# Weight halves, a fused mask and maximum, float32r sums of squares and a new order in a one-core hybrid decoder layer

## The chip, the cores and the metric

The kernel runs on one core of a Trainium2 chip. The metric is the device time of one execution in microseconds (us), as a median over runs. The engines are called as in the profile: PE (TensorE, matmuls), PEld (its weight loads), DVE (VectorE), ACT (ScalarE), POOL (GpSimd) and SP (SyncE, which here issues nearly all DMAs).

## What is computed

One decoder layer on 512 tokens of width 1024, all in float32. Cut to what matters:

```python
def swiglu(h, wg, wu, wd):
    return (jax.nn.silu(h @ wg) * (h @ wu)) @ wd          # inner width 2816
...
    x = x + 0.5 * swiglu(rms_norm(x, ffn1_norm), ffn1_wg, ffn1_wu, ffn1_wd)
    h = rms_norm(x, mix_norm)
    (q_n, kc, vc, ksl, vsl, kwn, vwn, gts, q_s, k_s, v_s) = jnp.split(h @ w_in, split_at, axis=-1)
    o_nsa = nsa_mixer(...)        # 8 heads: compressed + selected + window attention, gated, masked softmax
    o_sb = stick_breaking(q_s, k_s, v_s)                  # 8 heads, no softmax
    x = x + jnp.concatenate([o_nsa, o_sb], axis=-1) @ w_out
    x = x + memory_cross_attention(rms_norm(x, mem_x_norm), rms_norm(mem, mem_kv_norm), ...)   # 4 heads
    x = x + 0.5 * swiglu(rms_norm(x, ffn2_norm), ffn2_wg, ffn2_wu, ffn2_wd)
```

## The kernel before

Activations lie transposed in SBUF: eight tiles of 128 features by 512 tokens. A float32 operand is split into a high and a low float32r part: ACT copies the high part, DVE subtracts it from the source (`wsplit`, `split`), and a product is three float32r passes (`mm3`: high by high, high by low, low by high).

The work has three stretches. First comes a start written out by hand (`FIRST`): five plain blocks of the first feed-forward network (`ffn_up`) and the operands of its Winograd form (`right`: differences of the quarters b11, b12, b21, b22 of the activations). Then the rest of that network follows by `FEED["1"]`: a bare number f is one Winograd block of 128 inner columns (`wino_up`: seven products of 12 matmuls with 256 columns, four sums of weight quarters), `c.j` is a down step (`ffn_down`: group c of blocks into output tile j), and `name:i` is a store (`store_parts`: a weight unit that the middle will need is loaded, split and written to DRAM as parts). Groups of blocks are set by `GROUPS`. Then comes the middle by `MIDDLE` (projections, stick-breaking heads, NSA scores and outputs, memory attention, output projections, and `gate.f`, early halves of the second network's blocks), and last the second network by `FEED["2"]`.

None of this is issued in the order of the code. A `Planner` records every instruction with a cost in ns and its dependencies, and then lists them engine by engine by priority, under the limits of buffers and PSUM banks (`SYNC_NS`, `DMA_NS`, `ACT_MORE` and the `cost` function are its prices). Whatever it decides is the fixed order of each engine's queue. All instructions are issued from one line of `emit` (L498), so that the profile tells them apart by tile names: `raw` are weights as loaded, `w` split weights, `t` the tiles of 512, `p` PSUM, `d` parts in DRAM, `c` and `cr` constants (float32 and float32r), `s` small columns, `half` two intermediate sums of a Winograd block.

Places that the change touches: raw weights are loaded as tiles of 1024 columns, four buffers (`load`, `NRAW`); weight sums go into fresh `w` tiles (`comb` in `wino_up`); `norm_rstd` and `head_norm` sum squares over partitions with one float32 matmul by ones from `c`; `nsa_scores` adds the causal mask by a matmul of the identity with `R_NSM` and takes the maximum with `tensor_reduce` from PSUM; `cmp_mlp` builds the compression input in one raw tile and splits it in two halves of 512.

Of the kernel before, what the change touches and what calls it, by code (L numbers as in the profile page):

```python
# [81 lines left out]
MIDDLE = """sb_values rope sb_proj.2 sb_head.2.1 sb_proj.1 cmp_mlp.0 nsa_query.3 mem_norm sb_proj.3 sb_head.1.0  # L82
sb_head.3.1 nsa_query.0 sb_head.2.0 cmp_keys sb_head.1.1 sb_proj.0 sb_head.0.1 nsa_query.1 nsa_query.2 sb_head.3.0
query_rotate sb_head.0.0 nsa_key.0 nsa_key.1 key_rotate cmp_mlp.1 nsa_values nsa_compressed.3 nsa_compressed.1
nsa_scores.2.0 nsa_scores.1.0 nsa_scores.0.1 cmp_values nsa_scores.3.1 nsa_scores.0.0 nsa_compressed.2 wout_sb
nsa_out.1.0 nsa_scores.3.0 nsa_out.3.1 nsa_compressed.0 nsa_out.0.1 nsa_scores.1.1 nsa_out.3.0 nsa_out.0.0 mem_keys
nsa_out.1.1 nsa_out.2.0 mem_values nsa_scores.2.1 nsa_out.2.1 wout_nsa.0 mem_query.0.1 mem_query.0.0 mem_head.0.0.1
mem_head.0.0.0 mem_head.0.1.1 mem_head.0.1.0 mem_out.0 wout_nsa.1 right.0.3 right.0.0 mem_query.1.1 right.0.1
right.0.2 gate.11 mem_head.1.1.1 mem_query.1.0 mem_head.1.0.1 mem_head.1.0.0 mem_head.1.1.0 gate.16 gate.10 mem_out.1
gate.12 right.1.1 gate.9 gate.14 gate.8 gate.15 gate.13 gate.17 gate.19 right.1.3 gate.6 gate.18 gate.20 gate.1  # L90
right.1.0 right.1.2 gate.21"""
# [9 lines left out]
def _constants():  # L101
    c = np.zeros((P, N_CONST), np.float32)
    r = np.arange(P)
    c[:, C_ID:C_ID + P] = np.eye(P)
# [26 lines left out]
class Planner:  # L131
# [126 lines left out]
    def add_any(self, calls):  # L258
# [25 lines left out]
        if method == "dma_start":  # L284
# [3 lines left out]
            if out.tensor.name not in self.slots and ins[0].tensor.name in self.slots:  # L288
                op.nbytes *= self.STORE
# [211 lines left out]
class Kernel:  # L501
    def __init__(self, ctx, tc, xT, memT, pos, gains, const, conste, ws, wraw, pe, w2, out):
# [61 lines left out]
    def store_parts(self, name, i):  # L564
# [9 lines left out]

    def store_sums(self, f):

        rg, ru = self.load("2g", f), self.load("2u", f)
        self.stored["2s", f] = []

        def comb(x, y, op):  # L580
            t = self.comb(x, y, op)
            d = self.dp.tile([P, T], F32, tag=f"s{f}{len(self.stored['2s', f])}", name=self.name("d"))
            self.nc.sync.dma_start(d, t)
            self.stored["2s", f].append(d)
            return t

        s1 = comb(ru[:, :T], ru[:, T:], OP.add)
        s2 = comb(s1, rg[:, :T], OP.subtract)
        comb(rg[:, :T], ru[:, :T], OP.subtract)
        comb(rg[:, T:], s2, OP.subtract)  # L590

    def comb(self, x, y, op):
        nc = self.nc
# [1261 lines left out]
```

## Time and profile before

| | us |
|---|---|
| median of 3 runs | 1078.31 |
| lowest, highest | 1077.0, 1078.68 |
| the profiled execution | 1078.49 |
| its span, first to last instruction | 1076.7 |
| PE busy | 1054.0 |
| PEld busy | 954.4 |
| DVE busy | 898.3 |
| ACT busy | 651.6 |

The profile is of one execution. A row of a group reads: line, engine, operation, output and inputs by name, shapes and count, then the busy time of the group and the mean ns of one, then the idle time of the engine before them and what ended it. Busy times are unions, so that pipelined instructions overlap and the mean of one is longer than its share. A row of the timeline gives start, duration, the instructions merged into it, and in brackets the idle time before. The granted clock is a share of TensorE's full speed.

### The profile page before, as it was taken

The numbers are of one execution on the slowest core, as the hardware profiler recorded it, in microseconds if no ns is written. First come the engines' busy times: TensorE is split into PE (matmuls) and PEld (weight loads), VectorE is DVE, ScalarE is ACT, GpSimd is POOL, SyncE is SP. The second block draws the span as 40 slices with busy tenths as digits, with TensorE's granted clock in tenths as the row PEclk, the third lists the DMA queues.
The fourth block names the chain that finished last, engine by engine and source line by source line (L and its number), as shares of the span: only waits on it lengthen the run. The fifth ranks groups of instructions, "written<-read, shape, count | busy, mean of one in ns | idle before, by whom it ended". The sixth has DMA issues, their size and how long they took to land.

```text
span 1076.7 us, 18724 instructions
## 1 busy us (share of the span) xinstructions
PE 1054.0 (98%) x6740; PEld 954.4 (89%) x6740; DVE 898.3 (83%) x1848; ACT 651.6 (61%) x1355; POOL 49.7 (5%) x92
## 2 busy tenths in 40 slices
PE   9979999999999998999999999999999999999998
PEld 7869999998988887888788889999999999998987
DVE  6999898876958756789999988899999998874862
ACT  6656665544447547699858887878666554442430
POOL 0000000000000000000002642101000000000000
PEclk9989999999999999999989999999999999999999
DMA  7646455655655724501463233765343444342331
GB/s 249 183 161 207 166 176 196 216 177 167 226 182 171 270 89 137 188 24 47 136 219 114 69 119 125 229 197 166 118 123 113 138 137 138 137 136 80 113 113 69
DMA packets 64477, 162.08 MB, mean 151 GB/s; under 512 B 8064, under 2 KB 11520, under 8 KB 64384
## 3 DMA queue, kind: packets, MB, share of 16 engines
q1 hardware_dynamic: 63952, 160.59, 45.6%
q8 instruction: 53, 0.87, 0.3%
q14 instruction: 40, 0.33, 0.1%
q10 hardware_dynamic: 432, 0.29, 0.1%
HBM read 136.47 MB, written 23.07 MB: 148 GB/s over the span
## 4 chain that ended last, share of the span: by engine, by line
PE 81%; DVE 10%; DMA 4%; ACT 2%; issue 2%; SPq 0%; DVEq 0%; ACTq 0%
PE p L498 81%; DVE t L498 7%; DVE w L498 3%; DMA w<-d 2%; ACT t L498 2%; DMA d<-w 1%; DVE s L498 1%; DMA t<-t 0%; SPq L498 0%; ACT w L498 0%; DMA raw<-in_ws_dram 0%; DMA g<-in_gains_dram 0%; DVE raw L498 0%; ACT half L498 0%; DVEq L498 0%
## 5 line engine op out<-in xcount | busy, mean ns | idle before, releaser
L498 PE MATMUL p<-t,w 128*128 128x256 f32 (+1 forms) x5502 | 886.4, 320 | 10.7 <-ACT w L498 5.8
L498 PEld LDWEIGHTS p<-t,w 128*128 128x128 f32 x5502 | 784.6, 191 | 82.9 <-ACT w L498 6.5
L498 DVE TENSOR_TENSOR w<-raw,w 128x512 fp32r<-128x512 f32 (+1 forms) x372 | 240.8, 666 | 46.6 <-PE p L498 16.5
L498 ACT ACTIVATE t<-t 128x512 fp32r<-128x512 f32 (+9 forms) x409 | 207.9, 535 | 82.9 <-DVE t L498 70.6
L498 ACT ACTIVATE w<-raw 128x512 fp32r<-128x512 f32 (+1 forms) x333 | 192.5, 606 | 78.6 <-PE p L498 63.7
L498 DVE TENSOR_TENSOR t<-t,t 128x512 fp32r<-128x512 f32 (+7 forms) x339 | 188.2, 570 | 12.9 <-ACT t L498 8.7
L498 ACT ACTIVATE w<-w 128x512 fp32r<-128x512 f32 x156 | 96.6, 629 | 114.2 <-DVE w L498 104.1
L498 DVE TENSOR_TENSOR w<-w,w 128x512 fp32r<-128x512 f32 x156 | 104.8, 684 | 19.2 <-PE p L498 11.6
L498 ACT ACTIVATE t<-p 128x256 f32<-128x256 f32 (+5 forms) x158 | 76.7, 507 | 41.8 <-PE p L498 39.0
L498 PE MATMUL p<-t,t 128*128 128x512 f32 (+3 forms) x448 | 98.2, 333 | 1.1 <-DVE t L498 0.8
L498 DVE SCALAR_TENSOR_TENSOR t<-p,t 128x512 f32<-128x512 f32 (+3 forms) x107 | 66.3, 628 | 36.9 <-PE p L498 30.2
L498 DVE TENSOR_TENSOR t<-p,t 128x256 f32<-128x256 f32 (+5 forms) x159 | 82.3, 536 | 10.5 <-ACT t L498 5.9
L498 PEld LDWEIGHTS p<-t,t 128*128 128x128 f32 x448 | 70.6, 189 | 10.6 <-DVE t L498 2.3
L498 DVE TENSOR_TENSOR t<-p,half 128x256 f32<-128x256 f32 x117 | 45.6, 417 | 17.8 <-PE p L498 9.1
L498 ACT ACTIVATE t<-p,s,s 128x256 f32<-128x256 f32 (+3 forms) x80 | 47.6, 611 | 4.9 <-DVE s L498 3.8
L498 POOL TENSOR_SCALAR t<-t,s 128x256 f32<-128x256 f32 (+3 forms) x80 | 45.4, 588 | 104.5 <-DVE s L498 57.7
L498 PE MATMUL p<-w,t 128*128 128x512 f32 (+2 forms) x240 | 45.2, 335 | 0.0
L498 PE MATMUL p<-c,t 128*128 128x128 f32 (+3 forms) x264 | 40.5, 266 | 1.3 <-DVE t L498 1.0
L498 PEld LDWEIGHTS p<-w,t 128*128 128x128 f32 x240 | 37.4, 188 | 4.6 <-issue 0.5
L498 ACT ACTIVATE half<-p 128x256 f32<-128x256 f32 x46 | 17.3, 377 | 33.5 <-PE p L498 33.5
L498 PEld LDWEIGHTS p<-c,t 128*128 128x128 f32 x264 | 32.5, 152 | 5.6 <-issue 1.9
L498 DVE TENSOR_REDUCE s<-p 128x1 f32<-128x384 f32 (+3 forms) x52 | 32.4, 638 | 0.7 <-PE p L498 0.6
(77 smaller groups left out, 421.2 us busy)
## 6 DMA issues: line engine op xcount, KB each, us to landing
raw<-in_ws_dram SPq DMA_DIRECT2D x172, 512.0 KB, 4.1
w<-d SPq DMA_DIRECT2D x112, 256.0 KB, 3.5
d<-w SPq DMA_DIRECT2D x80, 256.0 KB, 4.1
raw<-in_ws_dram SPq DMA_DIRECT2D x16, 384.0 KB, 3.2
raw<-in_wraw_dram SPq DMA_DIRECT2D x8, 512.0 KB, 4.1
t<-in_xT_dram SPq DMA_DIRECT2D x8, 256.0 KB, 4.7
out_dram<-t SPq DMA_DIRECT2D x7, 256.0 KB, 2.0
raw<-in_ws_dram SPq DMA_DIRECT2D x4, 256.0 KB, 5.3
```

The source lines that it names most:

```text
L498: return getattr(getattr(self.nc, op.eng), method)(*args, **kw)
```

## The change

- **Halves.** Raw weights come as tiles of 512 columns, eight buffers, one DMA each. The start, `cmp_mlp` and the constants follow.
- **Sums in place.** Of the four weight sums of a Winograd block three are now written over the raw halves, as sums instead of differences. The operands change sign to match (`right` has two `scalar_tensor_tensor` steps), and so do the factors in `ffn_up` and `ffn_down`. A way to sum by DMA is in the code but not used, since `SUMS_BY_DMA` is empty.
- **Mask and maximum.** In `nsa_scores`, where one head fills a bank (query blocks 2 and 3), the mask matmul goes. One DVE instruction adds a mask tile to the PSUM scores, writes the result to SBUF and gives the row maximum; the exponential then reads SBUF.
- **Sums of squares.** `norm_rstd` (except the very first) and `head_norm` split the squares and sum them in two float32r passes; ones, block ones and identity move from `c` to `cr`.
- **Groups** of the first network are 6, 8, 8 instead of 8, 8, 6.
- **Order.** `FEED`, `MIDDLE`, `HOLD` and some of the planner's prices are new.

```diff
-NRAW, NW = 4, 15
+NRAW, NW = 8, 15
-LOOK, LOOK_DMA, LOOK_PARTS = 80, 400, 200
-ACT_MORE = 40
+LOOK, LOOK_DMA, LOOK_PARTS, LOOK_SUM = 80, 400, 200, 300
+ACT_MORE = 20
+SUMS_BY_DMA = ""
-NEG = -1e30
+NEG = -2.0 ** 100
-GROUPS = 8, 8, 6
-FEED = {"1": """cw:2 ws:3 cw:0 7 13 mo:1 15 wn:2 16 10 wn:0 6 8 cw:3 9 5 mo:0 0.6 17 cw:4 0.2 12 mq:0 19 0.0 mq:1 11
+GROUPS = {"1": (6, 8, 8), "2": (8, 8, 6)}
+FEED = {"1": """7 15 14 5 wn:3 20 8 0.1 ws:3 0.2 cw:1 0.5 10 mq:0 0.6 16 12 6 cw:4 0.7 cw:6 0.4 17 13 0.3 mq:1 11 0.0
...
-MIDDLE = """sb_values rope sb_proj.2 sb_head.2.1 sb_proj.1 cmp_mlp.0 nsa_query.3 mem_norm sb_proj.3 sb_head.1.0
+MIDDLE = """sb_values rope sb_proj.2 cmp_mlp.0 sb_proj.3 sb_proj.0 sb_head.0.1 sb_head.2.1 sb_head.3.1 cmp_keys
...
-    SYNC_PE_NS = 120
+    SYNC_PE_NS = 80
-    DMA_NS, DMA_GBPS, STORE = 1650, 245, 2
+    DMA_NS, DMA_GBPS, STORE = 2700, 300, 1.6
...
-        raw = self.wtile("raw", F32, NRAW, (P, 1024))
         self.nc.bias -= LOOK_DMA
-        self.nc.sync.dma_start(raw[:, start:w], self.ws[UNIT_AT[name] + i, :, start:w])
+        for h in halves:
+            raw[h] = self.wtile("raw", F32, NRAW)
+            n = min(w - h * T, T)
+            self.nc.sync.dma_start(raw[h][:, :n], src[:, h * T:h * T + n])
...
+    def column_sums(self, ps, ones, src):
+
+        w = src.shape[-1]
+        parts = [p[:, :w] for p in self.pair()]
+        self.split(src, *parts)
+        for i, p in enumerate(parts):
+            self.nc.tensor.matmul(ps, self.cr[:, ones:ones + P], p, start=i == 0, stop=i == 1)
...
-        self.nc.tensor.matmul(ps, self.c[:, C_ONE:C_ONE + P], acc, start=True, stop=True)
+            self.column_sums(ps, R_ONE, acc)
...
+        def negative(out, x, y):
+            nc.vector.scalar_tensor_tensor(out, x, -1.0, y, OP.mult, OP.subtract)
...
-        minus(t12[:, :H], b12, b11)
-        minus(t12[:, H:], b22, t12[:, :H])
+        minus(t12[:, :H], b11, b12)
+        negative(t12[:, H:], t12[:, :H], b22)
         minus(t34[:, :H], b22, b12)
-        minus(t34[:, H:], b21, t12[:, H:])
+        negative(t34[:, H:], t12[:, H:], b21)
...
-        s1 = comb(0, lambda: a21, lambda: a22, OP.add)
+        s1 = dma_sum(in_u[:, :T], in_u[:, T:]) if dma else add(a21, a22)
         self.prod(Y[:, H:], self.wsplit(a22), B, "t4")
-        s2 = comb(1, lambda: s1, lambda: a11, OP.subtract)
+        s3 = dma_sum(in_u[:, :T], in_g[:, :T]) if dma else add(a11, a21, a21)
+        s2 = add(s1, a11, a11)
...
-        nc.tensor.matmul(ps, self.c[:, C_BD:C_BD + P], sq, start=True, stop=True)
+        self.column_sums(ps, R_BD, sq)
...
-        for h in range(2):
-            t = self.wtile("raw", F32R, NRAW, (P, 1024))
-            src = A.rearrange("p g (n l) -> p g n l", l=16)[:, :, :, h * 8:(h + 1) * 8]
-            w = t.rearrange("p (l a g n) -> p a g n l", l=8, a=2, g=2)
-            self.split(src, w[:, 0], w[:, 1])
+        for h in range(4):
+            t = self.wtile("raw", F32R, NRAW)
+            w = t.rearrange("p (l a g n) -> p a g n l", l=4, a=2, g=2)
+            for g in range(2):
+                self.split(A[g].rearrange("p (n l) -> p n l", l=16)[:, :, h * 4:(h + 1) * 4], w[:, 0, g], w[:, 1, g])
...
-            nc.tensor.matmul(sv[:, :, qt * P:], self.cr[:, R_ID:R_ID + P],
-                             self.cr[:, None, R_NSM:R_NSM + P].to_broadcast([P, per, P]),
-                             start=False, stop=True, skip_group_check=True)
-            nc.vector.tensor_reduce(nm, sv, AX.X, OP.max, negate=True)
+            if per == 1:
+
+                nc.vector.tensor_tensor_reduce(t[:, :w], s[:, :w], self.mask(w), 1.0, NEG, OP.add, OP.max, nm)
+                sv = t[:, None, :w]
+            else:
+                nc.tensor.matmul(sv[:, :, qt * P:], self.cr[:, R_ID:R_ID + P],
+                                 self.cr[:, None, R_NSM:R_NSM + P].to_broadcast([P, per, P]),
+                                 start=False, stop=True, skip_group_check=True)
+                nc.vector.tensor_reduce(nm, sv, AX.X, OP.max, negate=True)
```

Where the order stands now, at two places. First, DVE right behind the hand-written start, before: `raw215` is unit cw:2, `raw224` ws:3, `raw233` cw:0 (three stores), `raw242` is block 7, the first Winograd block; `t168` to `t178` are operands of `right`.

```order
L498 TENSOR_TENSOR w221_299<-raw215_293,w220_298 128x512
L498 TENSOR_TENSOR w226_304<-raw224_302,w225_303 128x512
L498 SCALAR_TENSOR_TENSOR t168_246<-t10_88,gm_78,t39_117 128x256
L498 SCALAR_TENSOR_TENSOR t171_249<-t5_83,gm_78,t39_117 128x256
L498 SCALAR_TENSOR_TENSOR t144_222<-p137_215,t39_117 128x512
L498 TENSOR_TENSOR t170_248<-t168_246,t169_247 128x512
L498 TENSOR_TENSOR t144_222<-t144_222,t143_221 128x512
L498 TENSOR_TENSOR w230_308<-raw224_302,w229_307 128x512
L498 SCALAR_TENSOR_TENSOR t171_249<-t9_87,gm_78,t39_117 128x256
L498 TENSOR_TENSOR t50_128<-t144_222,t49_127 128x512
L498 TENSOR_TENSOR w235_313<-raw233_311,w234_312 128x512
L498 TENSOR_TENSOR w239_317<-raw233_311,w238_316 128x512
```

The same place now: `raw171` and `raw172` belong to the last plain block, `raw227` to `raw230` are the halves of block 7.

```order
L503 TENSOR_TENSOR w176_254<-raw172_250,w175_253 128x512
L503 TENSOR_TENSOR t53_131<-t137_215,t52_130 128x512
L503 TENSOR_TENSOR t181_259<-t179_257,t180_258 128x512
L503 SCALAR_TENSOR_TENSOR t182_260<-t5_83,gm_78,t43_121 128x256
L503 SCALAR_TENSOR_TENSOR t182_260<-t9_87,gm_78,t43_121 128x256
L503 TENSOR_TENSOR w238_316<-raw227_305,w237_315 128x512
L503 SCALAR_TENSOR_TENSOR t152_230<-p138_216,t43_121 128x512
L503 TENSOR_TENSOR t184_262<-t182_260,t183_261 128x512
```

No store's split stands between the plain blocks and block 7 any more; before there were six low parts of three stores (the five shown, and `w217` of cw:2 further up).

Second, PE in `nsa_scores`, before: `p1603` to `p1612` are the scores of four heads of query block 2, `cr` the mask; the other rows are a projection.

```order
L498 MATMUL p1603_1682<-t1516_1594,t1451_1529 128x384
L498 MATMUL p1603_1682<-cr_73 128x128
L498 MATMUL p1606_1685<-t1516_1594,t1453_1531 128x384
L498 MATMUL p1606_1685<-cr_73 128x128
L498 MATMUL p1609_1688<-t1516_1594,t1455_1533 128x384
L498 MATMUL p1609_1688<-cr_73 128x128
```

And PE's rows for a head of query block 3 now (`p1750`), among a projection's:

```order
L503 MATMUL p1818_1897<-t1488_1566,w1820_1899 128x512
L503 MATMUL p1750_1829<-t1627_1705,t1545_1623 128x512
L503 MATMUL p1750_1829<-t1628_1706,t1545_1623 128x512
L503 MATMUL p1818_1897<-t1536_1614,w1819_1898 128x512
L503 MATMUL p1818_1897<-t1537_1615,w1819_1898 128x512
```

DVE's rows for the same head, `t1753` being the mask tile and ISA the name under which the new instruction stands:

```order
L503 ISA t1752_1831,s1751_1830<-p1750_1829,t1753_1832 128x512
L503 ISA s1751_1830 128x1
L503 RECIPROCAL s1722_1801<-s1722_1801 128x8
L503 SCALAR_TENSOR_TENSOR s1751_1830<-s1751_1830,s1541_1619 128x1
L503 TENSOR_REDUCE s1883_1962<-t1881_1960 128x8
```

The mask's matmul is gone from PE; on DVE one instruction and a second, small one that reads out the maximum stand where a reduction stood.

More of the change, by code (lines that the diff above doesn't have):

```diff
@@ L83 @@
[L83 to L87, printed above, removed]
@@ L195, in cost @@
         src_psum = any(a.tensor.name in self.psum for a in ins)
+        if n >= 128 and any(a.ap[-1][0] >= 16 and a.ap[-1][1] > 1 for a in [out] + list(ins)):
+            n *= 1.75
         if eng == "tensor":
@@ L287, in add_any @@
                 op.nbytes *= s
-            if out.tensor.name not in self.slots and ins[0].tensor.name in self.slots:
+            if kw.get("accum_op") is not None or out.tensor.name not in self.slots and ins[0].tensor.name in self.slots:
                 op.nbytes *= self.STORE
@@ L573, in store_parts @@
             self.stored[name, i].append(there)
[L575 to L593, printed above, removed]
-        t = self.wtile("w", F32, NW)
-        nc.bias -= LOOK
-        nc.on("weight sum", "tensor_tensor", t, x, y, op)
-        nc.bias += LOOK
-        return t
     def unit(self, name, i=0):
@@ L613, in unit @@
         raw = self.load(name, i)
-        return [self.wsplit(raw[:, h * T:(h + 1) * T], pieces=2 if early and h == 0 else 1) for h in range(2)]
+        return [self.wsplit(raw[h], pieces=2 if early and h == 0 else 1) for h in range(2)]
     def unit_of(self, name, i):
@@ L742, in constants @@
     def constants(self):
[L743 to L745 removed]
+        for c in range(0, N_CONSTE, T):
+            n = min(N_CONSTE - c, T)
+            e = self.wtile("raw", F32, NRAW)[:, :n]
+            self.nc.sync.dma_start(e, self.conste_d[:, c:c + n])
+            self.nc.scalar.activation(self.cr[:, c:c + n], e, AF.Copy)
+        self.nc.vector.tensor_scalar(self.one, self.cf[:, R_ID:R_ID + 1], -0.5, None, OP.mult)
     def norm_block(self, src, gcol, hi, lo, acc, first):
@@ L891, in wino_up, with dma_sum, add @@
         early = gt is not None
-        there = self.stored.get((k + "s", f))
-        if not there or not early:
-            rg = self.load(k + "g", f)
-            a11, a12 = rg[:, :T], rg[:, T:]
-        ru = self.load(k + "u", f, T if there else 0)
-        a21, a22 = ru[:, :T], ru[:, T:]
-        def comb(n, x, y, op):
-            if not there:
-                return self.comb(x(), y(), op)
-            t = self.wtile("w", F32, NW)
-            nc.bias -= LOOK_PARTS
-            nc.sync.dma_start(t, there[n])
-            nc.bias += LOOK_PARTS
-            return t
+        a11, a12 = self.load(k + "g", f)
+        dma = k in SUMS_BY_DMA
+        in_g, in_u = [self.ws[UNIT_AT[k + n] + f] for n in "gu"]
+        def dma_sum(x, y):
+            t = self.wtile("raw", F32, NRAW)
+            nc.bias -= LOOK_SUM
+            nc.sync.dma_start(t, x)
+            nc.gpsimd.dma_start(t, y, accum_op=OP.add)
+            nc.bias += LOOK_SUM
+            return t
+        def add(x, y, out=None):
+            t = self.wtile("w", F32, NW) if out is None else out
+            nc.bias -= LOOK
+            nc.on("weight sum", "tensor_tensor", t, x, y, OP.add)
+            nc.bias += LOOK
+            return t
+        a21, a22 = self.load(k + "u", f, (1,) if dma else (0, 1))
         X, Y, Z = self.ps("mm")[:, :H], self.ps("at"), self.ps("at")[:, :H]
```

150 lines of the change are left out of this document (80 added, 70 removed).

## Prediction

> **What bounds the kernel now.** I read the page's totals first, then the engines by stage, then what TensorE (PE) waited for, then the groups of instructions by shape.
>
> ```profile
> span 1076.7 us, 18724 instructions
> PE 1054.0 (98%) x6740; PEld 954.4 (89%) x6740; DVE 898.3 (83%) x1848; ACT 651.6 (61%) x1355; POOL 49.7 (5%) x92
> ```
>
> TensorE is busy in all but 22.7 us. So time can go in three ways: less matmul work, less of those 22.7 us, or less time at half clock, which the busy figure hides. The profiled execution took 1078.49 us, 1.8 us around the span; the median of the runs is 1078.31. I sum against 1078.5. About 0.2% (2.2 us) is what a measurement of this kernel can tell from no change.
>
> The next view is the windows by stage: stretch, its length, then busy time (and count) of PE, PEld, DVE, ACT and POOL, then the granted clock, the DMA share and GB/s.
>
> ```profile
> 60.00:79.00 19.00, 12.34 (x68) 10.89 (x67) 19.00 (x40) 10.15 (x19) 0.00 (x0) 0.82 0.26 90
> 79.00:125.00 46.00, 44.30 (x360) 43.27 (x359) 41.20 (x76) 27.58 (x55) 0.00 (x0) 1.00 0.55 181
> 125.00:330.00 205.00, 205.00 (x1362) 189.23 (x1361) 165.24 (x297) 107.50 (x211) 0.00 (x0) 1.00 0.56 189
> 420.00:435.00 15.00, 11.51 (x71) 10.37 (x70) 11.68 (x18) 11.46 (x22) 0.00 (x0) 1.00 0.46 140
> 435.00:525.00 90.00, 89.41 (x464) 75.53 (x463) 78.70 (x184) 77.00 (x164) 1.28 (x2) 1.00 0.28 84
> 525.00:550.00 25.00, 23.57 (x120) 18.83 (x119) 23.65 (x40) 20.50 (x38) 0.00 (x0) 0.86 0.46 141
> 550.00:700.00 150.00, 147.75 (x1016) 134.62 (x1015) 136.98 (x372) 115.39 (x309) 44.11 (x78) 1.00 0.46 150
> 700.00:800.00 100.00, 99.43 (x814) 97.96 (x813) 97.40 (x228) 74.20 (x170) 4.10 (x8) 1.00 0.51 159
> 800.00:1060.00 260.00, 260.00 (x1745) 241.02 (x1745) 209.77 (x383) 115.78 (x202) 0.00 (x0) 1.00 0.36 119
> ```
>
> Two places stand out. From 60 to 79 us PE is idle for 6.7 us while VectorE (DVE) is busy for all 19.00 of 19: DVE is the bound there, and the clock falls to 0.82, which is 19 x 0.18 = 3.4 us of lost clock, part of it while PE was idle anyway. From 79 to 125 another 1.7 us go. This is the **front**: the first Winograd blocks of the first feed-forward network, right behind the hand-ordered start. The other place is the **middle**, 420 to 800 us: 3.5 + 0.6 + 1.4 + 2.3 + 0.6 = 8.3 us idle and 25 x 0.14 = 3.5 us of clock. From 125 to 330 and from 800 to 1060 PE never stops.
>
> The waits of PE from 50 to 125 us, longest first:
>
> ```profile
> PE p L498 <- ACT w L498: 5.2, 2, 3.6
> PE p L498 <- DVE t L498: 2.2, 3, 1.4
> PE p L498 <- DVE w L498: 0.8, 1, 0.8
> ```
>
> All are for split weights (w) or for the Winograd operands (t); the splits on ACT wait in turn for sums on DVE. None is for a DMA.
>
> **PE work that goes.** Two kinds. First, the 32 mask matmuls of 128 columns in `nsa_scores` for query blocks 2 and 3 (8 per call, 2 head groups, 2 blocks). The second kind is the exact-f32 matmul of the sums of squares, now two float32r passes. Timeline rows give the place that each takes in the queue:
>
> ```profile
> 576.10 0.22 PE L498 MATMUL p<-cr 128*128 128x128 f32 x1
> 576.16 0.39 PE L498 MATMUL p<-t,t 128*128 128x384 f32 x1
> ...
> 370.71 2.43 PE L498 MATMUL p<-w,t 128*128 128x512 f32 x10
> 372.98 1.02 PE L498 MATMUL p<-t,c 128*128 128x512 f32 x2
> 373.43 2.88 PE L498 MATMUL p<-w,t 128*128 128x512 f32 x10
> ```
>
> A mask holds the queue 0.06 us (start to start); its own 0.22 us is the upper end. 32 x 0.06 = 1.9 us, at most 7.0. I take 1.9, since the matmuls overlap. The f32 matmul of 512 columns holds 373.43 - 372.98 = 0.45 us, and the ten matmuls behind it take 2.88 instead of 2.43: 0.90 us in all.
>
> ```profile
> L498 PE MATMUL p<-t,w 128*128 128x256 f32 x3744 | 473.6, 285 | 9.2 <-ACT w L498 5.2 <-DVE t L498 3.0 <-DVE w L498 0.8
> L498 PE MATMUL p<-t,w 128*128 128x512 f32 x1758 | 426.7, 393 | 1.6 <-ACT t L498 0.8 <-ACT w L498 0.6
> ```
>
> A float32r pass costs 426.7 / 1758 = 0.243 us at 512 columns and 473.6 / 3744 = 0.126 at 256. So 0.41 us go at each of three places with 512 columns (the norm before the middle, two key norms). At five with 256 (memory norm, two halves before the second network, two memory keys) I take half of 0.90 for the old one: 0.45 - 0.25 = 0.20. Together 2.2 us. The first norm of all keeps its f32 matmul. Sum: **-4.1 us**, if PE is the bound where these stand.
>
> **The front.** The order now has none of the store splits ahead of the first Winograd block: in the rows above in the section on the change, three units (six low-part splits) stood on DVE before block 7. After them the old feed had nine blocks and five more stores before its first down step; the new one has six blocks and one store, since a first group of six is complete early.
>
> ```profile
> 399.35 1.29 DVE L498 TENSOR_TENSOR w<-raw,w 128x512 fp32r<-128x512 f32 x2
> ...
> L498 DVE TENSOR_TENSOR w<-raw,w 128x512 fp32r<-128x512 f32 x309 | 204.7, 683 | 36.9 <-ACT w L498 14.8 <-PE p L498 11.1 <-issue 7.7
> L498 DVE TENSOR_TENSOR t<-t,t 128x256 f32<-128x256 f32 x67 | 27.7, 416 | 0.2
> L498 DVE SCALAR_TENSOR_TENSOR t<-t,t 128x256 f32<-128x256 f32 x5 | 2.6, 513 | 0.2
> L498 DVE SCALAR_TENSOR_TENSOR t<-t,t 128x512 f32<-128x512 f32 x12 | 8.2, 685 | 0.1
> ```
>
> Two splits back to back take 1.29, one takes 0.683, so each further one adds 0.61 us: 6 x 0.61 = 3.7 us of DVE go from the stretch in which DVE was never idle. Against that stand eight operand steps that become SCALAR_TENSOR_TENSOR: 8 x (0.513 - 0.416) = 0.8 us. Net 2.9 us of the 6.7. The Trainium skill has a rule against this edit: "Vector Engine (DVE) Microarchitecture Reference", section "Points that are easy to get wrong", says that a scalar-tensor-tensor of two SBUF sources that are not bf16 runs at half rate. The last row is such an instruction with f32 sources, and its 685 ns are those of the plain tensor operation on 512 elements (683): the trace does not agree; by the rule the eight would cost 8 x 0.27 = 2.1 us instead of 0.8.
>
> From 79 to 125 us the five stores were ten splits, 6.1 us of DVE, more than the 1.7 us that PE lost: I take all 1.7. The half clock followed the idle stretch. PE ran 22 matmuls in 5.35 us from 72.89 on, where 22 x 0.126 = 2.8 us would do:
>
> ```profile
> 72.89 5.35 PE L498 MATMUL p<-t,w 128*128 128x256 f32 x22 [3.62 <-ACT w L498]
> ```
>
> 2.6 us were lost so. With 3.8 us of idle left it may stay: between 0 and 2.6, and I take 2.4, because the single wait of 3.62 us is what the 2.9 us cut. Front: 2.9 + 1.7 + 2.4 = **-7.0 us**; ends 3 and 10.8 (8.4 idle and all of the clock).
>
> **The middle** gets more DVE work. Its prices:
>
> ```profile
> L498 DVE TENSOR_REDUCE s<-p 128x1 f32<-128x512 f32 x16 | 10.6, 676 | 0.2 <-PE p L498 0.2
> L498 DVE TENSOR_REDUCE s<-p 128x1 f32<-128x384 f32 x16 | 8.4, 549 | 0.0
> L498 DVE TENSOR_TENSOR t<-p,t 128x512 f32<-128x512 f32 x8 | 5.4, 672 | 0.0
> L498 ACT ACTIVATION_READ_ACCUMULATOR t<-p,s,s 128x1 f32 x80 | 16.5, 206 | 0.0
> L498 DVE TENSOR_TENSOR t<-t,t 128x256 fp32r<-128x256 f32 x44 | 17.8, 415 | 1.2 <-ACT t L498 1.1
> ```
>
> The trace has no TENSOR_TENSOR_REDUCE. One pass over PSUM and SBUF is 672 ns, one reduction of the same width 676: if it streams once it costs what the reduction did, if it streams twice it adds 0.68 us (512) or 0.55 (384). I take once, as the nearest row does both reads in one pass. The order shows a second small instruction behind each, which reads the result out; the nearest row is ACT's own read, 0.21 us, so 0 to 32 x 0.21 = 6.6 us. Three splits of 512 (0.683) and five of 256 (0.415) for the float32r passes add 4.1 us, and as much on ACT. `cmp_mlp` splits 16 pieces of 128 instead of 4 of 512: by 683 ns at 512 and 416 at 256 an instruction's fixed part is 0.149 us, so 12 x 0.149 = 1.8 us more. Up to 12.5 us, against 11.3 + 1.4 + 13.0 + 2.6 = 28.3 us in which DVE idles from 435 to 800. That is cover on the average, not at 525 to 550 (23.65 of 25) or 700 to 800 (97.40 of 100). Their latency matters where a chain waits: the longest wait of the middle is the first `cmp_mlp`, where PE needs pieces that DVE and ACT make from a projection just finished.
>
> ```profile
> 426.01 2.73 DVE L498 SCALAR_TENSOR_TENSOR raw<-p,t 64x496 f32<-64x496 f32 x4 [1.01 <-PE p L498]
> ...
> 431.02 1.19 PE L498 MATMUL p<-w,raw 128*128 128x256 f32 x8 [3.50 <-issue]
> ```
>
> From 426.0 to 431.0 the chain takes 5 us, PE has 1.5 us of other work. In the new order the same ten score matmuls and three masks, and two more passes, stand between, so the wait stays near 3 us; the quarters save some of it. The rest of the middle is a new order throughout, with the same kind of waits; which of the 8.3 us idle and 3.5 us of clock remain can't be read from the order. I take no net change, with ends at -9 and +8.
>
> **Loads.** Raw weights come as two DMAs of 256 KB instead of one of 512.
>
> ```profile
> raw<-in_ws_dram SPq DMA_DIRECT2D x172, 512.0 KB, 4.1
> w<-d SPq DMA_DIRECT2D x112, 256.0 KB, 3.5
> ```
>
> A half lands in 3.5 us where the whole took 4.1, with as many bytes in flight, so nothing is added as long as they overlap; PE's waits above show none for raw weights. Sums written in place free three weight buffers for each block and hold raw halves a little longer: nothing, since PE stood still only where DVE was full.
>
> **Sum:** 1078.5 - 4.1 - 7.0 + 0 = 1067.4, so **1067 us**.
>
> **The rivals.**
> - *A, the forecast*: 1067, its own range 1060 to 1073. Chance 0.48.
> - *B, the middle becomes DVE's*: the 12.5 us of new DVE work meet the full stretches, the 4.1 us of PE are not gained, and 4 us more are lost: 1075. For it: 97.40 of 100 busy. Against: 28.3 us of slack. 0.13.
> - *C, the new order also clears the middle*: two thirds of 11.8 us go, 1067 - 8 = 1059. For it: most of those waits are for latency, which an order can cover. 0.20.
> - *D, slower*: TENSOR_TENSOR_REDUCE streams twice. 16 x 0.68 + 16 x 0.55 = 19.7 us of DVE in `nsa_scores`, where 550 to 700 us has 13.0 us of slack already half spent (6.6 + 4.1): 17 us show, 1084. It turns the change into a loss beyond 11 us, a mean above about 0.61 + 0.34 + 0.08 = 1.0 us for the 32. Against: 672 and 676. 0.09.
> - *E, the front does not do what the order suggests*: the wait there is for the operands of `right`, which stay, so only 2 of 7 us come: 1072. For it: 2.2 of the 8.2 us of waits are on DVE t. 0.08.
> - *F, halves come late*: the two halves land one behind the other, 7.0 instead of 4.1 us; a block of four halves then needs 14.0 us while its 84 matmuls of 0.126 take 10.6, and 39 blocks lose up to 3.4 us each: towards 1200. Against: PE waits for no raw weight. 0.02. The Trainium skill speaks for it: "DMA: Bandwidth & Descriptors", section "Bandwidth", asks for DMAs of 1 MiB and more; the rows, 4.1 and 3.5 us, agree that halving a load hardly shortens it, and no run here shows whether that matters.
>
> **How the numbers follow.** Faster by over 0.2% (below 1076.1): A 0.48, C 0.20, E 0.08, and 0.08 of B: 0.84. Slower (above 1080.5): D 0.08, F 0.02, 0.01 of B: 0.11. Within: 0.05. The range leaves out D, F and the outer parts of B and C, about 0.18: 1055 to 1077.
>
> **What would show it.** Right: from 60 to 79 us PE busy by some 3 us more and a clock above 0.9; p<-cr of 128 columns x16 instead of x48; no p<-t,c of 512 columns behind the first; the new DVE instruction near 0.68 us; no PE wait on raw weights. Wrong: DVE full and PE idle in the same window as before (E); PE idle above 13 us between 420 and 800 (B); the new instruction above 1.0 us (D); a wait on raw weights among PE's first five (F); under 4 us idle in the middle (C).

## The result and the profile after

The changed kernel takes 1068.84 us (median of 4 runs, 1066.2 to 1070.98) against 1078.12 before in the same session: a ratio of 0.9914, 95% interval 0.9889 to 0.9939. The forecast was 1067, range 1055 to 1077. The profiled execution took 1068.09.

The page's first lines after:

```profile
span 1066.3 us, 19290 instructions
PE 1046.8 (98%) x6708; PEld 946.7 (89%) x6708; DVE 908.9 (85%) x1904; ACT 653.3 (61%) x1376; POOL 49.0 (5%) x93
```

The span is shorter by 10.4 us. PE is busy for 7.2 us less, but idle (span less busy) for only 3.2 us less: 19.5 instead of 22.7. The windows by stage show where; columns as before:

```profile
60.00:79.00 19.00, 18.97 (x150) 18.41 (x149) 19.00 (x38) 11.73 (x24) 0.00 (x0) 1.00 0.29 85
79.00:125.00 46.00, 44.78 (x363) 44.01 (x363) 42.19 (x80) 28.13 (x56) 0.00 (x0) 1.00 0.54 173
125.00:330.00 205.00, 203.21 (x1333) 186.65 (x1333) 159.32 (x277) 106.84 (x203) 0.00 (x0) 1.00 0.64 209
330.00:420.00 90.00, 87.39 (x411) 73.05 (x410) 76.12 (x158) 57.55 (x120) 0.00 (x0) 1.00 0.69 224
420.00:435.00 15.00, 15.00 (x76) 12.53 (x75) 13.18 (x24) 10.58 (x20) 0.00 (x0) 1.00 0.39 125
435.00:525.00 90.00, 88.96 (x472) 74.62 (x470) 84.42 (x183) 84.91 (x182) 1.22 (x2) 1.00 0.21 60
525.00:550.00 25.00, 22.65 (x155) 21.77 (x155) 23.55 (x64) 11.73 (x28) 0.00 (x0) 0.86 0.73 236
550.00:700.00 150.00, 146.61 (x991) 130.84 (x991) 137.85 (x396) 123.17 (x327) 43.46 (x79) 1.00 0.44 141
700.00:800.00 100.00, 99.69 (x816) 98.38 (x816) 97.06 (x218) 71.22 (x163) 4.07 (x8) 1.00 0.47 143
800.00:1050.00 250.00, 248.81 (x1641) 228.73 (x1640) 198.21 (x360) 106.35 (x186) 0.00 (x0) 1.00 0.39 120
```

One row of the kernel before, from 330 to 420 us, is needed beside those of the prediction:

```profile
330.00:420.00 90.00, 89.19 (x420) 73.36 (x420) 62.39 (x116) 52.53 (x103) 0.00 (x0) 1.00 0.52 174
```

PE's idle time (length less busy) by stage, worked out from these rows and those before:

| stage | before | after |
|---|---|---|
| 60 to 125, the front | 8.4 | 1.3 |
| 125 to 420 | 0.8 | 4.4 |
| 420 to 435 | 3.5 | 0 |
| 435 to 800 | 4.8 | 7.1 |
| 800 to 1050 | 0 | 1.2 |

The front's hole is gone, and so is its half clock (0.82 to 1.00 over 19 us, 3.4 us at most). But 1.8 us of idle time opened from 125 to 330 us, where PE never stopped before. The hole at 420 only moved ahead of 420, with the compression step that makes it: 2.6 us from 330 to 420 now. So of 7.1 us of idle time that the front gave, the rest of the kernel took back more than half (3.9); what the whole gained is 3.2 us of idle time and 7.2 of busy time, of which the clock makes at most 3.4 and less matmul work at least 3.8.

A profile is one execution, and a small difference between two of them can be scatter. Three runs below (two steps, four masks, two float32 matmuls) keep each engine's order of the changed kernel and alter nothing ahead of 330 us. In their profiles PE is idle for 1.2, 2.6 and 3.2 us from 79 to 330 us, where this one has 3.0, and for 0 to 0.1 us from 800 to 1050, where this one has 1.2.

### The profile page after: what moved, and what is told of

Same layout as the page of the kernel before. It is cut to its first block, busy times and chain, and to the rows that moved or that the text cites. A ratio compares the mean times of both kernels' runs of the same rounds, so it can differ in the third digit from the quotient of the medians.

```text
span 1066.3 us, 19290 instructions
## 1 busy us (share of the span) xinstructions
PE 1046.8 (98%) x6708; PEld 946.7 (89%) x6708; DVE 908.9 (85%) x1904; ACT 653.3 (61%) x1376; POOL 49.0 (5%) x93
## 4 chain that ended last, share of the span: by engine, by line
PE 80%; DVE 11%; DMA 3%; ACT 3%; issue 2%; SPq 0%; ACTq 0%; DVEq 0%
PE p L503 80%; DVE t L503 7%; ACT t L503 2%; DMA raw<-in_ws_dram 2%; DVE s L503 2%; DVE w L503 2%; DMA d<-w 1%; DVE raw L503 0%; SPq L503 0%; DMA w<-d 0%; ACT w L503 0%; DVE gates L503 0%; DVE half L503 0%; ACTq L503 0%; ACT L498 0%
## 5 line engine op out<-in xcount | busy, mean ns | idle before, releaser
L503 PEld LDWEIGHTS p<-t,w 128*128 128x128 f32 x5502 | 781.8, 190 | 81.5 <-DVE t L503 10.4
L503 ACT ACTIVATE w<-raw 128x512 fp32r<-128x512 f32 (+1 forms) x450 | 266.7, 613 | 201.3 <-PE p L503 117.8
L503 DVE TENSOR_TENSOR w<-raw,w 128x512 fp32r<-128x512 f32 (+1 forms) x450 | 295.2, 672 | 66.2 <-issue 24.4
L503 DVE TENSOR_TENSOR t<-t,t 128x512 fp32r<-128x512 f32 (+8 forms) x332 | 187.1, 578 | 8.7 <-ACT t L503 5.8
L503 PE MATMUL p<-t,t 128*128 128x256 f32 (+4 forms) x450 | 100.7, 337 | 1.6 <-DVE t L503 1.3
L503 DVE SCALAR_TENSOR_TENSOR t<-p,t 128x512 f32<-128x512 f32 (+2 forms) x107 | 66.6, 629 | 33.6 <-PE p L503 32.2
L503 DVE TENSOR_TENSOR t<-p,t 128x256 f32<-128x256 f32 (+4 forms) x159 | 83.1, 537 | 8.0 <-ACT t L503 5.1
L503 DVE TENSOR_TENSOR raw<-raw,raw 128x512 f32<-128x512 f32 (+1 forms) x94 | 58.8, 635 | 0.9
L503 ACT ACTIVATE w<-w 128x512 fp32r<-128x512 f32 x39 | 24.3, 624 | 25.4 <-DVE w L503 13.6
L503 PE MATMUL p<-cr,t 128*128 128x128 f32 (+2 forms) x256 | 39.2, 265 | 0.0
L503 ACT ACTIVATE t<-t,g 128x256 fp32r<-128x256 f32 (+1 forms) x40 | 23.6, 590 | 21.8 <-DVE t L503 19.7
L503 PEld LDWEIGHTS p<-cr,t 128*128 128x128 f32 x256 | 31.8, 151 | 4.3 <-issue 0.5
```

The source lines that it names most:

```text
L503: return getattr(getattr(self.nc, op.eng), method)(*args, **kw)
```

## The experiments

Times are medians in us; a difference is against the changed kernel's 1068.84 unless another is named. Each ratio is against the kernel before, run on the same chip, with its 95% interval. Where a run isn't said to keep each engine's order, the planner made a new one for it, and the new order is part of what the run measures.

### The front

**The old feed and groups in the changed kernel:**

```diff
-GROUPS = {"1": (6, 8, 8), "2": (8, 8, 6)}
-FEED = {"1": """7 15 14 5 wn:3 20 8 0.1 ws:3 0.2 cw:1 0.5 10 mq:0 0.6 16 12 6 cw:4 0.7 cw:6 0.4 17 13 0.3 mq:1 11 0.0
+GROUPS = {"1": (8, 8, 6), "2": (8, 8, 6)}
+FEED = {"1": """cw:2 ws:3 cw:0 7 13 mo:1 15 wn:2 16 10 wn:0 6 8 cw:3 9 5 mo:0 0.6 17 cw:4 0.2 12 mq:0 19 0.0 mq:1 11
...
```

> The changed kernel with the feed and the groups (8, 8, 6) of the first network as before; everything else as changed. Theory (the front is DVE's: the store splits ahead of the first Winograd block starve PE): PE idle 4 to 7 us from 60 to 79 us again and the clock there below 0.9, so 7 to 10 us come back on 1068.8: 1076 to 1079. Rival 1 (the gain is in the edits of the code and in the middle's order): within 2.5 us of 1068.8. Rival 2 (in-place sums alone cure the front, since they free buffers): PE idle under 1 us from 60 to 79 us in spite of the old feed.

1075.46, ratio 0.998 [0.9968, 0.9991]: 6.6 us more.

```profile
60.00:79.00 19.00, 15.27 (x92) 13.95 (x91) 18.83 (x39) 10.22 (x19) 0.00 (x0) 0.82 0.32 105
```

3.7 us idle and the clock at 0.82: the front's loss is back, though smaller than before's 6.7, and a little under what the theory gave. Both rivals of this run fall.

**The same feed and groups in the kernel before** (its single tuple of groups made one per network):

> The kernel before with only the new feed and the groups 6, 8, 8 of the first network. Theory: the front's 7 to 10 us go without any other edit, 1078.1 becomes 1068 to 1071, PE idle under 1 us from 60 to 79 us, clock above 0.95 there. Rival 1: over 1075.

1112.23, ratio 1.0323 [1.0306, 1.034]: 34 us slower than before. The theory falls; its rival said only "over 1075", and no loss was expected by either.

```profile
60.00:79.00 19.00, 16.17 (x113) 15.10 (x112) 19.00 (x40) 10.14 (x20) 0.00 (x0) 0.91 0.25 74
...
125.00:330.00 205.00, 190.32 (x1258) 172.48 (x1257) 157.74 (x289) 105.26 (x205) 0.00 (x0) 1.00 0.55 189
330.00:420.00 90.00, 76.62 (x308) 60.34 (x307) 46.47 (x78) 36.36 (x65) 0.00 (x0) 0.91 0.60 205
```

The first window is better than before by 3.8 us, part of what the theory says (2.8 us of idle time and a clock of 0.91 are left). The next two lose 28.1 us. From 125 to 330 us PE waits for split weights and operands from DVE, and DVE, not even full (157.74 of 205), waits for PE. The waits of PE and then of DVE in that window:

```profile
PE p L498 <- DVE w L498: 7.5, 8, 2.1
PE p L498 <- DVE t L498: 6.3, 8, 0.9
```

```profile
DVE t L498 <- PE p L498: 29.0, 17, 4.8
```

The feed is not at fault by itself, since the changed kernel runs it; its order doesn't fit this code.

**Only the three stores moved in the kernel before:**

```diff
-FEED = {"1": """cw:2 ws:3 cw:0 7 13 mo:1 15 wn:2 16 10 wn:0 6 8 cw:3 9 5 mo:0 0.6 17 cw:4 0.2 12
+FEED = {"1": """7 13 mo:1 15 wn:2 16 10 wn:0 6 8 cw:3 9 5 mo:0 0.6 17 cw:2 cw:4 0.2 ws:3 12 cw:0
...
```

> The kernel before with only the three stores cw:2, ws:3 and cw:0 moved from the head of the first feed to behind its first down steps; blocks and groups as they were. Theory in its narrow form (six low parts of 0.61 us on DVE ahead of the first block are the cause): 5 to 8 us less than before, 1070 to 1073, and PE idle from 60 to 79 us under 2 us. Rival (groups of 6 or the order of the blocks is what helps): within 2.5 us of 1078.1. Rival E of the prediction (the wait is for the operands of right): PE idle from 60 to 79 us still over 4 us.

1092.89, ratio 1.0138 [1.0124, 1.0152]: slower by 15 us.

```profile
60.00:79.00 19.00, 16.55 (x100) 15.17 (x99) 18.70 (x38) 8.89 (x19) 0.00 (x0) 0.82 0.17 56
...
125.00:330.00 205.00, 193.57 (x1254) 176.59 (x1253) 155.71 (x274) 100.48 (x193) 0.00 (x0) 0.99 0.60 203
```

Again the first window gains: 4.2 us of PE, with 2.5 us still idle and the clock still at 0.82. So the splits of the three stores are most of what held PE there, and not the operands of `right`; but 11.4 us of idle time open behind the window, and for the whole time the theory and both rivals fall.

**Three stores put first in the changed kernel:**

```diff
-FEED = {"1": """7 15 14 5 wn:3 20 8 0.1 ws:3 0.2 cw:1 0.5 10 mq:0
+FEED = {"1": """wn:3 ws:3 cw:1 7 15 14 5 20 8 0.1 0.2 0.5 10 mq:0
...
```

> The changed kernel with three stores (wn:3, ws:3, cw:1) moved to the head of the first feed. Theory: 4 to 8 us more than 1068.8, that is 1073 to 1077, with PE idle over 3 us from 60 to 79 us. Rivals (groups, or the code): within 2.5 us of 1068.8.

1070.12, ratio 0.9928 [0.9916, 0.994]: 1.3 us more, which the intervals don't separate from none.

```profile
60.00:79.00 19.00, 15.00 (x91) 13.99 (x91) 18.32 (x36) 10.18 (x20) 0.00 (x0) 0.82 0.26 86
79.00:125.00 46.00, 46.00 (x384) 45.93 (x383) 42.08 (x79) 27.86 (x55) 0.00 (x0) 1.00 0.34 108
125.00:330.00 205.00, 204.28 (x1351) 188.01 (x1350) 158.79 (x276) 107.43 (x205) 0.00 (x0) 1.00 0.59 196
```

Three stores do starve PE: 4.0 us idle and the clock at 0.82 in the first window, as predicted. But the stores' work is then not done later, and 79 to 330 us has 0.7 us idle, less than any of the four profiles of the changed kernel's order (1.2 to 3.2). The mechanism in the window is right, its price for the whole is not the window's. Of the 6.6 us that the old feed costs, most is therefore the rest of the feed and the groups; these runs don't part the two.

### Code and order, each alone

**All edits of the code with before's feeds, groups, middle, holds and prices:**

> All edits of the code as changed, but the feeds, groups, middle, holds and planner's prices as before. Theory after the first four runs (the code's edits give the PE work and half of the front by themselves, and the order only the rest): 1069 to 1074, with PE idle of 3 to 5 us from 60 to 79 us. Rival (an order fits only the code that it was made for, whichever it is): over 1080, with waits of PE in places where neither kernel has any.

**The code before with all the new tables:**

> The code as before, but the feeds, groups, middle, holds and planner's prices as changed. Theory (the new feed needs what the code frees): like the run with the new feed alone, over 1095, with more than 20 us of PE idle from 125 to 420 us. Rival 1 (the prices make the new feed fit): 1068 to 1078. Rival 2 (the new middle gains on its own): at least 8 us less than the 1112 of the new feed alone.

| | tables before | tables after |
|---|---|---|
| code before | 1078.1 | 1082.99, ratio 1.0053 [1.0034, 1.0073] |
| code after | 1091.36, ratio 1.0126 [1.0112, 1.0141] | 1068.84 |

Neither half gains anything by itself; each alone is slower. Of the first run's two theories the rival holds (over 1080). Of the second run's the theory (over 1095) and rival 1 (1068 to 1078) fall. Rival 2's figure is met, 29 us less than the 1112 of the new feed alone where it asked for 8, but by the windows below not for its reason, the new middle. The code with the old tables:

```profile
60.00:79.00 19.00, 13.70 (x69) 12.18 (x68) 18.13 (x38) 8.61 (x16) 0.00 (x0) 0.73 0.28 100
...
550.00:700.00 150.00, 143.93 (x921) 126.64 (x921) 134.29 (x392) 113.95 (x297) 37.89 (x68) 0.98 0.43 142
```

The front is bad again (5.3 us idle and a clock of 0.73, where the kernel before has 6.7 and 0.82), and from 550 to 700 us PE loses 6.1 us instead of 2.3. The old code with the new tables:

```profile
60.00:79.00 19.00, 18.77 (x146) 17.98 (x145) 19.00 (x38) 12.02 (x24) 0.00 (x0) 1.00 0.31 99
...
125.00:330.00 205.00, 201.71 (x1313) 183.23 (x1312) 170.95 (x308) 111.94 (x219) 0.00 (x0) 1.00 0.62 210
330.00:420.00 90.00, 84.67 (x377) 70.18 (x377) 52.78 (x93) 46.02 (x85) 0.00 (x0) 0.94 0.58 202
```

Here the front is clean in the old code: the tables clear it by themselves. With the new feed but the old prices and middle, PE was busy for 16.17 us from 60 to 79 us, now for 18.77; so 2.6 us of that window come with the tables behind the feed, the planner's prices most likely, for which the prediction had no term. From 125 to 420 us it had 28.1 us idle, now 8.6, which is 19.5 of the 29 us between these two runs. The old code still pays there, and has none of the saved PE work.

### Which edit of the code lets the new feed run

**Fresh weight sums instead of sums in place:**

```diff
-        s3 = dma_sum(in_u[:, :T], in_g[:, :T]) if dma else add(a11, a21, a21)
+        s3 = dma_sum(in_u[:, :T], in_g[:, :T]) if dma else add(a11, a21)
-        s2 = add(s1, a11, a11)
+        s2 = add(s1, a11)
-        s4 = add(a12, s2, a12)
+        s4 = add(a12, s2)
```

> The changed kernel with the four weight sums of a Winograd block in fresh weight buffers again instead of three of them in place; all else as changed. Theory (in-place sums free three of fifteen weight buffers for each block, and the new feed lives on that): over 10 us of PE idle from 125 to 420 us, 1080 or more. Rival (halves in eight buffers, or the prices, are what the feed lives on): within 4 us of 1068.8.

1065.0, ratio 0.9878 [0.986, 0.9897]: 3.8 us *less*. My theory of the weight buffers falls; the rival's "within 4 us" is just met, on the fast side. This is the fastest version of all, and its interval only just overlaps that of the changed kernel [0.9889, 0.9939].

```profile
125.00:330.00 205.00, 205.00 (x1340) 188.27 (x1339) 161.38 (x279) 109.08 (x207) 0.00 (x0) 1.00 0.63 216
330.00:420.00 90.00, 87.39 (x404) 73.07 (x403) 75.65 (x158) 57.90 (x121) 0.00 (x0) 0.98 0.65 212
```

The new idle time of both networks (1.8 and 1.2 us) is gone; from 800 to 1050 us PE is busy for all 250. Only the first of the two can be put down to the sums: the second is also gone in the three runs that keep the order with sums in place. From 79 to 330 us the two profiles with fresh sums (this one and the run with masks below) have 0 and 0.6 us idle, the four with sums in place and the changed kernel's order 1.2 to 3.2. What such a wait is shows in the changed kernel's timeline before its first one behind 125 us:

```profile
145.57 0.63 ACT L503 ACTIVATE w<-raw 128x512 fp32r<-128x512 f32 x1 [2.17 <-DMA d<-w]
...
146.24 0.69 DVE L503 TENSOR_TENSOR w<-raw,w 128x512 fp32r<-128x512 f32 x1 [2.11 <-DMA d<-w]
146.84 0.69 DVE L503 TENSOR_TENSOR w<-raw,raw 128x512 f32<-128x512 f32 x1
147.44 0.75 DVE L503 TENSOR_TENSOR t<-p,half 128x256 f32<-128x256 f32 x2
...
147.92 0.86 PE L503 MATMUL p<-t,w 128*128 128x256 f32 x5 [1.19 <-DVE t L503]
```

ACT and DVE stand for 2.1 us until a store's DMA has left a weight buffer. The step that PE needs, `t<-p,half`, comes two instructions behind on DVE, and PE waits 1.19 us. It is tempting to blame such waits on the sums in place. PE's wait and ACT's three that matter from 125 to 330 us, in the changed kernel:

```profile
PE p L503 <- DVE t L503: 3.0, 3, 1.2
ACT w L503 <- DMA d<-w: 16.6, 12, 2.3
ACT w L503 <- DVE raw L503: 13.8, 8, 3.9
ACT w L503 <- DVE w L503: 10.2, 4, 6.0
```

And with fresh sums, where PE's list has no matmul that waits for DVE:

```profile
ACT w L503 <- DVE w L503: 35.7, 25, 7.3
ACT w L503 <- DMA d<-w: 11.4, 10, 2.2
```

With fresh sums ACT waits less for stores, but longer for the sums (35.7 instead of 13.8 + 10.2 = 24.0). And in the run with two steps below, whose sums are in place, the waits for stores are 11.8 us as well. So ACT's waits don't tell the two versions apart. The pair of runs shows that the version with fresh sums is faster; which wait makes `t<-p,half` late with sums in place is open, and so is what part of the 3.8 us the new order has in it.

**Whole weight tiles again, four buffers, one DMA each:**

```diff
-NRAW, NW = 8, 15
+NRAW, NW = 4, 15
...
-        for h in halves:
-            raw[h] = self.wtile("raw", F32, NRAW)
-            n = min(w - h * T, T)
-            self.nc.sync.dma_start(raw[h][:, :n], src[:, h * T:h * T + n])
+        self.nc.sync.dma_start(raw[:, :w], src[:, :w])
...
```

> The changed kernel with raw weights as whole tiles of 1024 columns again, four buffers and one DMA each (the start, the constants and the compression's pieces likewise); sums still in place, all else as changed. Theory (the new feed lives on buffers that come free by halves): from 125 to 420 us PE is idle over 8 us instead of 4.4, 1076 to 1090. Rival (the prices of the planner are what makes the feed fit, the halves do nothing): within 3 us of 1068.8.

1075.44, ratio 0.9977 [0.9967, 0.9987]: 6.6 us more.

```profile
125.00:330.00 205.00, 201.60 (x1314) 184.90 (x1313) 167.56 (x298) 112.20 (x220) 0.00 (x0) 0.99 0.61 208
330.00:420.00 90.00, 84.78 (x397) 69.71 (x396) 59.51 (x119) 47.79 (x95) 0.00 (x0) 1.00 0.64 219
```

8.6 us idle from 125 to 420 us, over 8 as the theory says and the same 8.6 as the old code with the new tables; the time is just under the theory's 1076, and the rival falls. So halves in eight buffers are what lets the new feed run, and the prediction gave them nothing. That it is because buffers come free by halves is not shown: besides the compression's, PE's longest waits there with whole tiles are for operands and split weights (2.4, 1.4 and 1.1 us for DVE `t`, DVE `w` and ACT `w`), and none is for a load.

### The prices of the middle and of PE's work

**The fused instruction as two steps, each engine's order kept:**

```diff
+        if method == "tensor_tensor_reduce":
+            t, s, m, nm = args[0], args[1], args[2], args[7]
+            self.nc.vector.tensor_tensor(t, s, m, OP.add)
+            return self.nc.vector.tensor_reduce(nm, t, AX.X, OP.max)
```

> The changed kernel, each engine's order kept, with the fused instruction replaced at its place by two: an addition of the mask and a maximum over the sum. That is what the fused one would cost if it streamed twice: 16 x 0.68 + 16 x 0.55 = 19.7 us more of DVE from 435 to 800 us. By rival D's sum 17 us of it show: 1086. By slack on DVE (18.6 us idle from 435 to 800 us, and the head of DVE's queue late only in places) a third to a half shows: 1075 to 1079. If PE is covered throughout: within 2.5 us of 1068.8.

1087.1, ratio 1.009 [1.0075, 1.0106]: 18.3 us more. The extra work is less than the 19.7 us of the expectation, since the fused instruction's read-out goes: DVE is busy for 925.3 us in all instead of 908.9, 16.4 more. So all of it comes through.

```profile
550.00:700.00 150.00, 134.53 (x820) 114.35 (x820) 134.17 (x344) 107.22 (x283) 41.11 (x76) 0.97 0.34 110
```

PE's wait in this window that heads the list is for the addition:

```profile
PE p L507 <- DVE t L505: 8.4, 17, 0.8
```

Rival D's 17 us hold. DVE's idle time in the middle is no cover (by the changed kernel's rows it is 22.1 us from 435 to 800; the 18.6 of the expectation was a slip of mine): PE is idle for 15.5 us here instead of 3.4, although DVE is busy for only 134.17 of 150.

**Masks as matmuls again, on top of the fresh sums** (the code of `nsa_scores` before, planned anew):

> The changed kernel with fresh weight sums and with the masks as matmuls and the maxima as reductions from PSUM again. The run with two steps showed DVE as the bound from 550 to 700 us. On DVE a head then costs 0.68 + 0.15 us instead of 0.68 + 0.08 + 0.21, so 32 x 0.14 = 4.5 us less, and PE gets 32 x 0.06 = 1.9 us more. Theory (DVE bounds there, the fused instruction costs more than it saves): 1.5 to 4 us below the 1065.0 of fresh sums alone. Rival (the prediction's own term, PE bounds there): 2 us above it, 1067. No difference within 1.5 us: the two cancel.

1068.79, ratio 0.9917 [0.9904, 0.993]: 3.8 us more than with fresh sums alone. The theory that DVE's 4.5 us decide falls; the rival has the sign right, with 2 us too little.

```profile
525.00:550.00 25.00, 20.24 (x134) 18.91 (x134) 24.77 (x67) 14.79 (x31) 1.83 (x3) 0.80 0.60 190
550.00:700.00 150.00, 148.62 (x1017) 134.17 (x1016) 133.45 (x354) 119.78 (x323) 39.19 (x73) 1.00 0.45 145
```

From 550 to 700 PE's idle time is 1.4 us instead of 3.0 with fresh sums alone, so DVE's relief is there. From 525 to 550, where no mask of 128 columns stands, it is 4.8 instead of 2.8, and the clock 0.80 instead of 0.86: that comes with the new order and not with the masks. So the run doesn't say what the masks alone cost; the next one does.

**The mask's matmul four times ahead of each fused instruction, order kept:**

```diff
+        if method == "tensor_tensor_reduce":
+            s, n = args[1], args[1].shape[-1]
+            for _ in range(4):
+                self.nc.tensor.matmul(s[:, n - P:], *self.masks, start=False, stop=True, skip_group_check=True)
...
```

> The changed kernel, each engine's order kept, with the mask's matmul of 128 columns put back four times ahead of each fused instruction, 128 matmuls in all. The prediction's price (0.06 us each, start to start): 7.7 us, 1076.5, if PE is the bound there. By a mask's own time (0.22 us each): 28 us, 1097. If DVE bounds the stretch: under 4 us, below 1073.

1080.86, ratio 1.0033 [1.002, 1.0046]: 12.0 us for 128 matmuls, 0.094 us each, give or take a quarter by the two intervals. Their row gives 17.9 / 128 = 0.14 us of busy time each, part of it beside their neighbours:

```profile
L506 PE MATMUL p<-cr 128*128 128x128 f32 x128 | 17.9, 262 | 0.0
```

So the 32 masks were worth some 3.0 us, if one costs a quarter of four in a row: between the 1.9 and 7.0 us that 0.06 and 0.22 us each would give.

**Sums of squares by two float32 matmuls each, order kept:**

```diff
+        if "again" in kw:
+            i, ones, hi = kw["again"]
+            if i:
+                return
+            for _ in range(2):
+                self.nc.tensor.matmul(args[0], ones, hi, start=True, stop=True, skip_group_check=True)
+            return
...
```

> The changed kernel, each engine's order kept, with the two float32r passes of each sum of squares replaced by two float32 matmuls over the high part alone (the low part is split but left out). By the prediction's prices (0.90 us a float32 matmul of 512 columns against 0.49 for two passes, 0.45 against 0.25 at 256) the doubled matmuls add 3 x 1.31 + 5 x 0.65 = 7.2 us: 1076. By the time from the start of one to the next alone (0.455 and 0.245 us) 2.5 us: 1071.3. If PE waits at these places for other work anyway: within 1.5 us of 1068.8.

1070.27, ratio 0.9927 [0.9908, 0.9945]: 1.4 us more, by the two intervals between some 2 less and 5 more. So the 7.2 us fall; 2.5 and nothing are not told apart. Yet on PE the price was near the predicted 0.90 and 0.45: each matmul stands twice in these rows, so 5.7 / 6 = 0.95 us at 512 columns and 5.3 / 10 = 0.53 at 256. (A ninth sum, of 64 columns, takes part too; the prediction counts eight.)

```profile
L508 PE MATMUL p<-t,cr 128*128 128x512 f32 x12 | 5.7, 601 | 0.0
L508 PE MATMUL p<-t,cr 128*128 128x256 f32 x20 | 5.3, 387 | 0.5 <-ACT t L510 0.5
```

The stretch around the second compression, where two of the doubled sums at 512 columns stand, differs in one thing:

```profile
525.00:550.00 25.00, 22.71 (x146) 19.06 (x145) 23.51 (x60) 14.10 (x30) 0.00 (x0) 1.00 0.55 183
```

The clock is 1.00 there instead of 0.86, which is 3.5 us of clock. The three other profiles of this order (changed kernel, two steps, four masks) all have 0.86. PE's idle time is not shorter, 2.3 us against 2.4, so the matmuls don't fill the wait. That they keep the clock up, and that this is why little of their price arrives, is a guess from one profile.

## Why the prediction was right, and where its steps failed

The time was right within 2 us, and the mechanism of the front was right where it was shown. That the sum came so close is partly luck, since its errors cancelled: the front gave 7.1 us of idle time instead of 2.9 + 1.7 = 4.6, the rest of the kernel took back 3.9 instead of nothing, and two terms put at nothing, the halves and the sums in place, each move the time by several us.

- **PE work, -4.1.** The total fits (at least 3.8), the split does not. The masks, put at 1.9 by 0.06 us each, measured 3.0 by repetition. The sums of squares, put at 2.2, can't be seen in the time: by the same prices two float32 matmuls for each should have cost 7.2 us, and cost 1.4, though each matmul was as long as predicted. "-4.1 us, if PE is the bound where these stand" was the condition, and at the second compression, where PE is idle for 2.3 us of 25, it is not the bound.
- **The front, -7.0.** What would show it came in full: PE busy by 6.6 us more from 60 to 79 us, clock 1.00. Idle time and clock give 7.1 + 3.4 = 10.5 us at most, near the upper end of 10.8 (by its own terms, 8.4 + 2.6, that end is 11.0). The size of 2.9 us came from six splits alone; moving the three stores gave 4.2 in the old code, and the tables behind the feed another 2.6. The step that failed is to take a window's gain for the kernel's. Stores put back first cost the window 4 us and its clock, but the kernel 1.3, not told from none.
- **Sums in place, "nothing, since PE stood still only where DVE was full".** This failed: the version without them is 3.8 us faster, and with them PE waits for DVE from 125 to 330 us, where it had never stopped. Which wait ahead of DVE's step causes it stays open. Three of four in place is the part of the change to leave out first.
- **Loads, "nothing is added as long as they overlap".** Nothing was added, but the term had the wrong sign: halves in eight buffers gain 6.6 us in the new order. The landing was not the point (3.1 us for a half, no PE wait on raw weights).

```profile
raw<-in_ws_dram SPq DMA_DIRECT2D x364, 256.0 KB, 3.1
```

- **The middle, 0.** Idle time from 420 to 800 us is 7.1 us against 8.3, the dip at 525 to 550 is the same 0.86; counting the first compression, which now stands ahead of 420, it is 9.7. No large net change is right; the cover that the text counted on is not. New DVE work was less than the 12.5 us feared (6.2 more busy from 435 to 800, with the first compression now ahead of it, and 10.6 in all). The fused instruction streams once, as assumed, and its read-out takes 2.5 us instead of up to 6.6:

```profile
L503 DVE CUSTOM_DVE_ANT_0 t<-p,t 128x512 f32<-128x512 f32 x16 | 10.6, 677 | 0.1
L503 DVE CUSTOM_DVE_ANT_0 t<-p,t 128x384 f32<-128x384 f32 x16 | 8.5, 549 | 0.0
L503 DVE DVE_READ_ACCUMULATOR2_ANT s<- 128x1 f32 x32 | 2.5, 79 | 0.0
L503 PE MATMUL p<-cr 128*128 128x128 f32 x16 | 3.9, 244 | 0.0
```

Had it streamed twice, the 18.3 us of the run with two steps are near what rival D said (17; the slack that D calls half spent is by its own figures 10.7 of 13.0, and the 17 follows from what is left). The last row is the sixteen masks that stay.

- **The wait at `cmp_mlp`, "near 3 us".** It is 2.6; the chain from DVE's first step to PE's matmul takes 4.4 us instead of 5.0:

```profile
397.65 2.75 DVE L503 SCALAR_TENSOR_TENSOR raw<-p,t 64x496 f32<-64x496 f32 x4
...
402.06 0.72 PE L503 MATMUL p<-w,raw 128*128 128x256 f32 x4 [2.61 <-issue]
```

- **The rivals.** A held. B and C fall: neither did the middle take 4 us more, nor did it clear. D falls with the new instruction at 677 and 549 ns. E falls: PE waits for one operand in 50 to 125 us (1.2 us), though `right` is still there. F falls: no wait on raw weights is on PE's list. What no rival named is that the order only pays with the code and the code only with the order.

Open is how the rest of the new feed, the groups and the planner's prices share what the tables gave: they were run together or in part only.

## What to carry to other kernels

Where a planner or a search has fixed every queue, an edit and its order are one change: run the 2 x 2 of code and tables before giving either the credit. A gain read in one window is not yet the kernel's: twice a window gained some 4 us and the kernel lost 15 and 34, each time with the new idle time right behind the window. So price such a move at the end of the kernel and not at the end of the window. And idle time of an engine is cover only where its queue can be ahead: 22 us of DVE's slack hid none of 16.4 us of added work.

## What the runs showed of the hardware

- A store's DMA that frees a buffer late holds ACT and DVE at the head of their queues: 12 waits of up to 2.3 us on ACT from 125 to 330 us, whose rows say `DMA d<-w`, though PE's list there shows only a DVE operand.
- A float32 matmul keeps PE busy for 0.95 us at 512 columns and 0.53 at 256, where two float32r passes take 0.49 and 0.25. Yet eighteen of them (two of only 64 columns) in place of as many passes cost 1.4 us in the end, not separable from none.
- DVE's read of an accumulator takes 79 ns, where ACT's took 206 in the kernel before.
- A mask matmul of 128 columns costs 0.094 us of the kernel's time, give or take a quarter, by adding 128 of them.
